# Three of eight pairs of k tiles by seven block products, two of a quad's weight sums made by adding transfers, banks kept open between chunks

## The chip, the cores and the metric

One NeuronCore of a Trainium2 chip runs the whole program. The metric is device time in microseconds (us), the median of several executions. One more execution is taken with the hardware profiler; the rows below are from that one. TensorE multiplies, VectorE (DVE) and ScalarE (ACT) do the elementwise work, GpSimd (POOL) does little, and SyncE (SP) issues most transfers.

## The reference

The reference is an encoder of two layers on 256 tokens of width 2048, in float32. Each layer has three mixers side by side (a chunked mLSTM, a latent attention, a dilated attention), an output projection, and a feed-forward part:

```python
x = x + jnp.einsum('bse,ed->bsd', y, w_out)
h = rms_norm(x, norm_ff)
u = jax.nn.relu(jnp.einsum('bsd,df->bsf', h, w_ff1))
return x + jnp.einsum('bsf,fd->bsd', u * u, w_ff2)
```

`w_ff1` is 2048 x 8192 and `w_ff2` is 8192 x 2048 in each layer. The change lies in the product with `w_ff2`.

## The kernel before

**Products.** Float32 values are split in two parts of a shorter format, hi and lo, and a product of two of them is three matmuls (hi hi, hi lo, lo hi). The main shape is a 128 x 128 stationary tile of activations with 512 columns of weights moving; the result goes to a PSUM bank of 512 columns. All of these go through the helper `mm` (L200).

**Weights.** The class `Weights` streams all weights in one fixed order (`weight_order`). An item is a 128 x 1024 tile: two k tiles of 128 rows by 512 columns. `load` sends it from HBM into one of three `wst` buffers on SP's queue (L239). `split` makes `whi` (an ACT copy) and `wlo` (a DVE subtraction) in one of four pairs of buffers, and `next` hands them to the matmuls in order, with the splits up to two items ahead. A load into a buffer waits on SP until the item that was in it is split.

**The order of the work** is written out by a planner (`Stream`): it keeps a clock that runs with the matmuls, gives every instruction of the side tasks a cost and a due time, and issues a task's next step between two matmuls when it is due (`pump`). It decides the order of instructions in each engine's queue, nothing else; at run time an engine takes its queue in order and waits for what each instruction needs.

**The feed-forward part** runs in four chunks of 2048 inner columns. A chunk has a first half (FF1: 16 tiles of `w_ff1`, two items each, with `ff1_end` for the activation) and a second (FF2: the product with its part of `w_ff2`). The 16 k tiles of FF2 make eight pairs `kp`, the outputs make four groups `g` of 512 columns, and two groups are done together, `left` and `right`, for both token tiles. Fast chunks (three of layer 0, four of layer 1; `fast`) do pairs 2 and 5 (`FAST`) in another way: the 256 x 256 block of activations and the 256 x 1024 block of weights are cut in 2 x 2, and seven products with sums of blocks take the place of eight. I call this a quad. Its activation sums come from `act_sums` in FF1. Its weights are two loaded items, "first" (the pair of the left group) and "second" (that of the right), and two made ones, "sums" and "more sums": four sums of 512 columns, made by four DVE additions (tile `ws`) in `split`. Of the seven products four go to banks of their own (`fast`, L200), the others straight to left and right. `fast_end` adds those four to the x tiles, with eight DVE additions and an ACT copy; then `ff2_end` adds left and right.

The order in a group pair was: left 0, 1, quad 2, left 3, 4, quad 5, left 6, 7, then right 0, 1, 3, 4, 6, 7.

Of the kernel before, what the change touches and what calls it, by code (L numbers as in the profile page):

```python
# [10 lines left out]
F32 = mybir.dt.float32  # L11
F32R = mybir.dt.float32r
AF = mybir.ActivationFunctionType
ALU = mybir.AluOpType
# [53 lines left out]

MLA_AT = ((3, 2), (3, 3), (3, 7), (4, 3), (5, 0), (6, 1))
MARGIN = 0.3  # L70
ML_AT_ONCE = 2
WARM = 14

# [148 lines left out]
class Weights:  # L222
# [2 lines left out]

    def __init__(self, c, items):
        self.c, self.items = c, items
        self.srcs = [(i, src, n) for i, (src, n, kind) in enumerate(items) if src is not None]
        self.st, self.hl = {}, {}
        self.i = self.d = self.k = 0  # L230

    def load(self):
        c = self.c
        if self.d == len(self.srcs):
            return
        i, src, n = self.srcs[self.d]
        self.st[i] = c.wp.tile([P, 1024], F32, tag="wst", name="wst", bufs=c.B_ST)
        for cols in self.pieces(i):
            c.nc.sync.dma_start(self.st[i][:, cols], src[:, cols])  # L239
        self.d += 1  # L240

    def pieces(self, i):

# [3 lines left out]
    def split(self):  # L247

        c, nc, k = self.c, self.c.nc, self.k
        src, n, kind = self.items[k]  # L250
        hi = c.wp.tile([P, 1024], F32R, tag="whi", name="whi", bufs=c.B_HL)
        lo = c.wp.tile([P, 1024], F32R, tag="wlo", name="wlo", bufs=c.B_HL)
        if kind == "sums":
            a, b = self.st.pop(k - 2), self.st.pop(k - 1)

            x, y = (c.big.tile([P, 1040], F32, tag="big", name="ws") for _ in range(2))
            self.st[k + 1] = y
            pieces, st = [slice(0, 512), slice(512, 1024)], x
        else:
            st = self.st[k] if kind else self.st.pop(k)  # L260
            if kind == "second":
                st = st[:, 512:]
                pieces = [slice(0, 512)]
            elif kind == "more sums":
                st = self.st.pop(k)
                pieces = [slice(0, 512), slice(512, 1024)]
            else:
                pieces = self.pieces(k)

        def parts():  # L270
            if kind == "sums":
                t1, t2, t3, t4 = x[:, :512], x[:, 512:1024], y[:, :512], y[:, 512:1024]
                for out, p, q in ((t3, b[:, :512], b[:, 512:]), (t1, a[:, :512], b[:, :512]), (t2, t3, a[:, :512]),
                                  (t4, t2, a[:, 512:])):
                    nc.vector.tensor_tensor(out=out, in0=p, in1=q, op=ALU.add)
                yield
            for cols in pieces:
                nc.scalar.copy(hi[:, cols], st[:, cols])
            yield
            for cols in pieces:  # L280
                nc.vector.tensor_tensor(out=lo[:, cols], in0=st[:, cols], in1=hi[:, cols].bitcast(F32),
                                        op=ALU.subtract)

        t = c.s.spawn(parts())
        if kind != "more sums":
            c.s.step(t)
        else:
            t.due = max(t.due, self.sums.due)
        if kind == "sums":
            self.sums = t  # L290
        self.hl[k] = (hi, lo, t)
        self.k += 1

    def next(self):
        while self.k < min(len(self.items), self.i + self.c.B_HL - 1):
            loads = self.items[self.k][0] is not None
            self.split()
            if loads:
                self.load()
        hi, lo, t = self.hl.pop(self.i)  # L300
        self.c.s.finish(t)
        self.i += 1
        return hi, lo

FAST = (2, 5)


def fast(l, ch, depth):  # L310
    return l == depth - 1 or ch < NCHUNK - 1


def weight_order(c, depth):
    srcs = []
    for l in range(depth):
        for g in range(9):
            for kp in range(KT // 2):
                if g == 1:
                    srcs.append((c.w_in1[l, kp], 2 * G1_W))  # L320
                else:
                    srcs.append((c.w_in[l, g - (g > 1), kp], 1024))
                srcs += [(c.w_mla[l, h], 832) for h, at in enumerate(MLA_AT) if at == (g, kp)]
        srcs += [(c.w_out[l, g, kp], 1024) for g, kps in OUT_ORDER for kp in kps]
        for ch in range(NCHUNK):
            srcs += [(c.w_ff1[l, ch * KT + i, half], 1024) for i in range(KT) for half in range(2)]
            if not fast(l, ch, depth):
                srcs += [(c.w_ff2[l, ch, g, kp], 1024) for g in range(NX) for kp in range(KT // 2)]
                continue
            for g in range(0, NX, 2):  # L330
                for kp in range(KT // 2):
                    if kp in FAST:
                        srcs += [(c.w_ff2[l, ch, g, kp], 1024, "first"), (c.w_ff2[l, ch, g + 1, kp], 1024, "second"),
                                 (None, 1024, "sums"), (None, 1024, "more sums")]
                    else:
                        srcs.append((c.w_ff2[l, ch, g, kp], 1024))
                srcs += [(c.w_ff2[l, ch, g + 1, kp], 1024) for kp in range(KT // 2) if kp not in FAST]
    return [(*a, None)[:3] for a in srcs]


# [232 lines left out]
def layer_tables(c):  # L573

    nc = c.nc
    vec = c.vec
    rope = c.cp.tile([P, 4, NT, MLA_ROPE], F32, tag="rope", name="rope", bufs=1)
    drope = c.cp.tile([P, 2, NT, 4, DIL_ROT], F32, tag="drope", name="drope", bufs=1)
    cs64 = c.const[:, C_C64:C_C64 + 2 * NT * MLA_ROPE].rearrange("p (a t d) -> p a t d", a=2, t=NT)
    cs32 = c.const[:, C_C32:C_C32 + 2 * NT * DIL_ROT].rearrange("p (a t d) -> p a t d", a=2, t=NT)  # L580
    for i in range(4):
# [82 lines left out]
def k_rope(c, z1):  # L664
# [15 lines left out]
    for tt in range(NT):  # L680
        transpose(c, tp[:MLA_ROPE, tt * P:(tt + 1) * P], kr[:, tt])

    kh = c.cp.tile([P, S], F32R, tag="krh", name="krh", bufs=1)
    kl = c.cp.tile([P, S], F32R, tag="krl", name="krl", bufs=1)
    nc.scalar.activation(kl[MLA_ROPE:], c.const[MLA_ROPE:, :S], AF.Copy, scale=0.0)
    yield
    k = tp[:MLA_ROPE, :S]
# [203 lines left out]
def ml_gates(c, z1):  # L891
# [57 lines left out]
                                 op0=ALU.min, op1=ALU.min)  # L949
    yield  # L950

    ahl = c.cp.tile([P, 2, S], F32R, tag="ml_ahl", name="ml_ahl", bufs=1)
    A2 = A.unsqueeze(1).to_broadcast([64, 2, S])
    nc.scalar.copy(ahl[:64], A2)
    nc.vector.tensor_tensor(out=ahl[64:], in0=A2, in1=ahl[:64].bitcast(F32), op=ALU.subtract)
# [167 lines left out]

def mixers(c, prepare, after):
    nc, s = c.nc, c.s
    dv = c.cp.tile([P, 2 * NT * DIL_H * DIL_DH], F32R, tag="dv", name="dv", bufs=1)
    dv = dv.rearrange("p (i t d) -> p i t d", i=2, t=NT)
    c.dv = {(i, tt): dv[:, i, tt] for i in range(2) for tt in range(NT)}
# [95 lines left out]
def ffn(c, l, last_layer, depth):  # L1224

    nc = c.nc
    nxt = [None] * KT
    c.xss = new_ss(c)
    for ch in range(NCHUNK):
        us = [None] * KT  # L1230
        quick = fast(l, ch, depth)
# [4 lines left out]
        for f in range(KT):  # L1236
# [4 lines left out]
            c.s.spawn(ff1_end(c, ps, f, us, uf[kp][:, i * S:(i + 1) * S] if kp in uf else None))  # L1241
            if i and kp in uf:
                c.s.spawn(act_sums(c, us, kp, uf[kp], hls, sums))
        for g in range(0, NX, 2):
            last = last_layer and ch == NCHUNK - 1 and g == NX - 2
            if quick:
                fast_groups(c, us, sums, l, ch, g, last, last_layer, nxt)
                continue
            for gg in (g, g + 1):
                ps = two_banks(c)  # L1250
# [22 lines left out]
    sums[kp] = [(hl[:, i * P:(i + 1) * P], hl[:, 512 + i * P:512 + (i + 1) * P]) for i in range(4)]  # L1273


def fast_groups(c, us, sums, l, ch, g, last, last_layer, nxt):

    def u(kt, tt):
        return us[kt][:, tt * P:(tt + 1) * P], us[kt][:, S + tt * P:S + (tt + 1) * P]
# [6 lines left out]

    one, two = slice(0, 512), slice(512, 1024)
    left, right = two_banks(c), None
    banks = None
    for kp in range(KT // 2):  # L1290
        if kp not in FAST:
            token_group(c, us, left, 512, [kp])
            continue
        first, end = kp == FAST[0], kp == FAST[-1]
        if first:
            right = two_banks(c)
            c.s.until(lambda: c.s.room["m"] >= 4)
            c.s.give(m=-4)
            banks = [new_bank(c, "fast") for _ in range(4)]
        p1, q5, p6, p7 = banks  # L1300
        c.s.until(lambda: kp in sums)
        s1, s2, s3, s4 = sums[kp]
        w = c.w.next()
        product(p1, u(2 * kp, 0), w, one, first, end)
        product(left[0], u(2 * kp + 1, 0), w, two, False, False)
        w = c.w.next()
        product(right[0], s4, w, one, first, False)
        w = c.w.next()
        product(q5, s1, w, one, first, end)
        product(p6, s2, w, two, first, end)  # L1310
        w = c.w.next()
        product(p7, s3, w, one, first, end)
        product(left[1], u(2 * kp + 1, 1), w, two, False, False)
        if end:
            done = c.s.spawn(fast_end(c, banks, g))
    c.s.spawn(ff2_end(c, left, g, l, ch, last_layer, nxt, done))
    kps = [kp for kp in range(KT // 2) if kp not in FAST]
    token_group(c, us, right, 512, kps[:-1] if last else kps, opened=(0,))
    if last:
        last_unit(c, us, right, 512)  # L1320
    c.s.spawn(ff2_end(c, right, g + 1, l, ch, last_layer, nxt, done))


def fast_end(c, banks, g):
# [265 lines left out]
```

## Time and profile before

| | |
|---|---|
| median of 3 runs | 2104.84 us (2104.66 to 2107.78) |
| the profiled execution | 2104.86 us, of which the span from first to last instruction is 2103.1 us |
| busy: PE, DVE, ACT, POOL | 2092.9, 1583.1, 1127.3, 14.0 us |
| moved | 389.91 MB, 185 GB/s on average |

The profile's page gives busy times of the engines, the DMA queues and the chain of waits that ended last. PE is TensorE's matmuls, PEld its weight loads. A stage is read by asking for the busy times of a stretch of the span; a wait is put down to the instruction that came last.

### The profile page before, as it was taken

How to read it: one execution, taken by the hardware profiler on the slowest of the kernel's cores; microseconds unless marked ns; L12 is line 12 of the kernel's file. 1: busy time of each engine (PE TensorE's matmuls, PEld its weight loads, DVE VectorE, ACT ScalarE, POOL GpSimd, SP SyncE). 2: the span in 40 equal slices, each digit the busy share in tenths (PEclk: the TensorE clock that was granted, in tenths of full speed). 3: DMA queues.
4: the chain of work that ended last, by engine and by line, in shares of the span. 5: the costliest groups of instructions: out<-in, count | busy, mean ns of one | idle time of the engine just before them, and what ended most of it. 6: DMA issues, size and time to landing. Idle time of an engine off the chain costs nothing.

```text
span 2103.1 us, 29314 instructions
## 1 busy us (share of the span) xinstructions
PE 2092.9 (100%) x10800; PEld 1790.8 (85%) x10800; DVE 1583.1 (75%) x2624; ACT 1127.3 (54%) x1870; POOL 14.0 (1%) x35
## 2 busy tenths in 40 slices
PE   9999999999999999999999999999999999999999
PEld 8888888888888888888888888888888888888887
DVE  6788865788778778765557888667887787787787
ACT  6777654454455444544456675554544554554453
POOL 1000000000000000001000000000000000000000
PEclk9999999999999999999999999999999999999999
DMA  7554455666656665666555445556666566666665
GB/s 259 167 173 153 150 171 180 194 189 204 191 183 200 200 191 183 210 192 199 179 172 171 139 139 160 175 180 192 192 204 191 179 205 202 186 191 207 187 194 180
DMA packets 109151, 389.91 MB, mean 185 GB/s; under 512 B 12368, under 2 KB 12496, under 8 KB 108752
## 3 DMA queue, kind: packets, MB, share of 16 engines
q1 hardware_dynamic: 107136, 384.71, 58.3%
q10 hardware_dynamic: 1872, 3.33, 0.4%
q8 instruction: 84, 1.38, 0.3%
q14 instruction: 59, 0.48, 0.1%
HBM read 385.90 MB, written 2.10 MB: 184 GB/s over the span
## 4 chain that ended last, share of the span: by engine, by line
PE 96%; DVE 1%; DMA 1%; ACT 1%; issue 0%; ACTq 0%; DVEq 0%
PE g L200 86%; PE fast L200 4%; PE mla_z L200 2%; DMA wst<-w_in 1%; PE oT L200 1%; DVE wlo L104 1%; PE mla_s L200 1%; ACT whi L104 1%; PE ml_h L200 1%; PE pT L206 1%; PE xT L206 0%; PE dil_s L200 0%; PE nkT L206 0%; PE dqkT L206 0%; PE ml_w L200 0%
## 5 line engine op out<-in xcount | busy, mean ns | idle before, releaser
L104 DVE TENSOR_TENSOR wlo<-wst,whi 128x1024 fp32r<-128x1024 f32 (+3 forms) x733 | 864.0, 1189 | 128.1 <-ACT whi L104 126.1
L104 ACT CAST whi<-wst 128x1024 fp32r<-128x1024 f32 (+3 forms) x733 | 748.9, 1024 | 394.0 <-DMA wst<-w_ff 154.1
L200 PE MATMUL g<-whi,u 128*128 128x512 f32 x1712 | 539.1, 389 | 0.0
L200 PE MATMUL g<-xg,whi 128*128 128x512 f32 x2048 | 489.8, 391 | 0.0
L200 PEld LDWEIGHTS g<-xg,whi 128*128 128x128 f32 x2048 | 376.4, 188 | 72.8
L200 PEld LDWEIGHTS g<-whi,u 128*128 128x128 f32 x1712 | 321.4, 188 | 66.7
L200 PE MATMUL g<-whi,xg 128*128 128x512 f32 (+1 forms) x1152 | 370.4, 388 | 0.5 <-ACT whi L104 0.5
L200 PE MATMUL g<-wlo,u 128*128 128x512 f32 x856 | 333.0, 389 | 0.0
L200 PEld LDWEIGHTS g<-xg,wlo 128*128 128x128 f32 x2048 | 262.8, 191 | 11.8 <-ACT xg L104 2.0
L200 PE MATMUL g<-xg,wlo 128*128 128x256 f32 x2048 | 267.3, 283 | 1.1 <-ACT xg L104 1.1
L200 PEld LDWEIGHTS g<-whi,xg 128*128 128x128 f32 x1152 | 214.3, 188 | 37.7 <-ACT whi L104 0.6
L200 PE MATMUL g<-wlo,xg 128*128 128x512 f32 (+1 forms) x576 | 220.8, 383 | 2.5 <-DVE wlo L104 2.5
L104 ACT COPY junk<-g 128x256 f32<-128x256 f32 x128 | 47.8, 374 | 303.5 <-PE g L200 303.5
L200 PEld LDWEIGHTS g<-wlo,u 128*128 128x128 f32 x856 | 160.7, 188 | 33.1
L104 DVE TENSOR_TENSOR junk<-g,junk 128x256 f32<-128x256 f32 x128 | 54.4, 425 | 172.4 <-ACT junk L104 172.4
L200 PE MATMUL g<-whi,y 128*128 128x512 f32 x512 | 164.5, 394 | 0.0
L200 PEld LDWEIGHTS g<-wlo,xg 128*128 128x128 f32 x576 | 108.6, 189 | 21.2 <-DVE wlo L104 4.8
L200 PEld LDWEIGHTS g<-whi,y 128*128 128x128 f32 x512 | 96.2, 188 | 19.5
L200 PE MATMUL g<-wlo,y 128*128 128x512 f32 x256 | 99.8, 390 | 0.0
L104 DVE TENSOR_TENSOR x<-g,x 128x512 f32<-128x512 f32 x80 | 53.4, 688 | 53.7 <-PE g L200 53.7
L104 ACT CAST whi<-ws 128x512 fp32r<-128x512 f32 x112 | 64.0, 619 | 41.1 <-PE g L200 41.1
L104 DVE TENSOR_TENSOR wlo<-ws,whi 128x512 fp32r<-128x512 f32 x112 | 71.6, 688 | 3.3 <-ACT whi L104 1.1
(244 smaller groups left out, 1694.6 us busy)
## 6 DMA issues: line engine op xcount, KB each, us to landing
wst<-w_ff SPq DMA_DIRECT2D x512, 512.0 KB, 4.2
wst<-w_in SPq DMA_DIRECT2D x127, 512.0 KB, 3.7
wst<-w_out SPq DMA_DIRECT2D x64, 512.0 KB, 4.2
wst<-w_in SPq DMA_DIRECT2D x16, 336.0 KB, 3.0
wst<-w_mla SPq DMA_DIRECT2D x12, 416.0 KB, 3.1
x<-x SPq DMA_DIRECT2D x2, 1024.0 KB, 6.5
out<-x ACTq DMA_DIRECT2D x8, 256.0 KB, 2.4
xt<-xT SPq DMA_DIRECT2D x7, 256.0 KB, 6.0
```

The lines of the kernel that those rows point to most:

```text
L104: return fn(*args, **kw)
L200: c.nc.tensor.matmul(out, lhsT, rhs, start=start, stop=stop)
L206: c.nc.tensor.transpose(out, src, c.ident[:n, :n])
```

## The change

- `FAST` becomes (1, 3, 5), three quads in a group pair. The order in the pair is written out (`FAST_ORDER`): left 0, quad 1, left 2, right 0, quad 3, left 4, right 2, quad 5, left 6, 7, right 4, 6, 7.
- A quad's two blocks are loaded in four halves into tiles of the pool `big`, arranged so that w11 and w22 are "first" and w12 and w21 "second". Plain loads keep the three `wst` buffers for themselves. Pairs are loaded up to 12 items (`AHEAD`) ahead of the split, at most two at a time.
- Of the four sums two (t1, t3) are made by transfers: SP loads w22 once more into a half of a `mix` tile, and two transfers issued by POOL add a second block from HBM to what is in the buffer. DVE makes the other two (t2, y) with two additions, due ten us (`LANDING`) after the loads on the planner's clock.
- The sums' tiles take the place of tiles that are free in the feed-forward part: the rope tables, the latent attention's shared keys and one mLSTM tile now lie in the same buffers, `mix0` and `mix1`; y uses the two `mla_zs` buffers.
- The groups' order alternates between chunks (0, 2 and 2, 0). Where a chunk ends with the group pair that the next begins with, the four quad banks stay open (`held`) and `fast_end` runs once for both. This is so at five places (two in layer 0, three in layer 1).
- The left group's output addition waits for `fast_end` only in the last chunk.

```diff
+LANDING = 10.0
+AHEAD = 12
...
+        if kind == "second":
+            self.sum[i] = t = c.s.spawn(self.add(i, self.items[i - 1][0], src))
+            c.s.step(t)
+            t.due = c.s.clk + LANDING
+
+    def loads(self):
+        while self.pairs and self.pairs[0][0] < self.k + AHEAD and self.out["pair"] < 2:
+            self.load(self.pairs)
+            self.load(self.pairs)
+        while self.plain and self.out["plain"] < self.c.B_ST:
+            self.load()
+
+    def add(self, i, first, second):
+        nc = self.c.nc
+        a, b = self.st[i - 1], self.st[i]
+        self.mix = 1 - getattr(self, "mix", 1)
+        x = self.c.cp.tile([P, 1024], F32, tag=f"mix{self.mix}", name="ws", bufs=1)
+        y = self.c.zp.tile([P, 2 * WZ], F32, tag="mla_zs", name="ws")[:, :512]
+        t1, t2, t3 = b[:, :512], x[:, :512], x[:, 512:]
+        nc.sync.dma_start(t3, first[1])
+        nc.gpsimd.dma_start(t1, first[0], accum_op=ALU.add)
+        nc.gpsimd.dma_start(t3, second[0], accum_op=ALU.add)
+        self.st[i + 1], self.st[i + 2] = (t1, t3), (t2, y)
+        yield
+        nc.vector.tensor_tensor(out=t2, in0=t3, in1=a[:, :512], op=ALU.add)
+        nc.vector.tensor_tensor(out=y, in0=t2, in1=b[:, 512:1024], op=ALU.add)
...
-                for out, p, q in ((t3, b[:, :512], b[:, 512:]), (t1, a[:, :512], b[:, :512]), (t2, t3, a[:, :512]),
-                                  (t4, t2, a[:, 512:])):
-                    nc.vector.tensor_tensor(out=out, in0=p, in1=q, op=ALU.add)
...
-FAST = (2, 5)
+FAST = (1, 3, 5)
+FAST_ORDER = ('l0', 'b1', 'l2', 'r0', 'b3', 'l4', 'r2', 'b5', 'l6', 'l7', 'r4', 'r6', 'r7')
...
+def pairs_order(l, ch, depth):
+    return (2, 0) if ch % 2 and fast(l, ch, depth) else (0, 2)
+
+def goes_on(l, ch, g, depth):
+    return (ch + 1 < NCHUNK and fast(l, ch, depth) and fast(l, ch + 1, depth) and pairs_order(l, ch, depth)[1] == g
+            and pairs_order(l, ch + 1, depth)[0] == g)
...
+            first, end = kp == FAST[0], kp == FAST[-1] and not hold
+            if first:
+                right = two_banks(c)
+                if banks is None:
+                    c.s.until(lambda: c.s.room["m"] >= 4)
+                    c.s.give(m=-4)
+                    banks = [new_bank(c, "fast") for _ in range(4)]
+            new = first and held is None
...
+            w = c.w.next()
+            product(p1, u(2 * kp, 0), w, one, new, end)
+            product(right[0], s4, w, two, first, False)
+            w = c.w.next()
+            product(left[0], u(2 * kp + 1, 0), w, one, False, False)
+            w = c.w.next()
+            product(q5, s1, w, one, new, end)
+            product(p7, s3, w, two, new, end)
+            w = c.w.next()
+            product(p6, s2, w, one, new, end)
+            product(left[1], u(2 * kp + 1, 1), w, two, False, False)
```

## Rows read from the trace of the kernel before

**Rows 1.** The page: busy us (share of span) x instructions; granted clock by slice.
```profile
PE 2092.9 (100%) x10800; PEld 1790.8 (85%) x10800; DVE 1583.1 (75%) x2624; ACT 1127.3 (54%) x1870; POOL 14.0 (1%) x35
...
PEclk9999999999999999999999999999999999999999
```

**Rows 2.** The page: shares of the chain that ended last, by engine and by line.
```profile
PE 96%; DVE 1%; DMA 1%; ACT 1%; issue 0%; ACTq 0%; DVEq 0%
PE g L200 86%; PE fast L200 4%; PE mla_z L200 2%; DMA wst<-w_in 1%; PE oT L200 1%; DVE wlo L104 1%; PE mla_s L200 1%; ACT whi L104 1%; PE ml_h L200 1%; PE pT L206 1%; PE xT L206 0%; PE dil_s L200 0%; PE nkT L206 0%; PE dqkT L206 0%; PE ml_w L200 0%
```

**Rows 3.** Waits of TensorE, whole run: for whom, us in total, times, longest us.
```profile
PE g L200 <- DVE wlo L104: 2.5, 4, 0.9
```

**Rows 4.** Busy us by stage: FF1 and FF2 of a chunk, its first group pair.
```profile
core 0: us, PE busy (x) PEld busy (x) DVE busy (x) ACT busy (x) POOL busy (x), PEclk, DMA share, GB/s
357.00:446.60 89.60, 89.04 (x517) 78.63 (x516) 66.78 (x112) 44.99 (x69) 0.00 (x0) 1.00 0.61 187
446.60:531.00 84.40, 84.40 (x374) 69.91 (x373) 70.60 (x90) 42.28 (x52) 0.00 (x0) 1.00 0.65 201
446.60:488.80 42.20, 42.20 (x188) 34.95 (x187) 35.05 (x46) 21.52 (x27) 0.00 (x0) 1.00 0.66 200
```

**Rows 5.** The chain in order of time, 440 to 510 us: start, us, what.
```profile
454.25 2.04 PE fast L200 x9
...
464.45 2.04 PE fast L200 x9
...
496.41 2.04 PE fast L200 x9
```

**Rows 6.** Groups by shape in one group pair's FF2: busy us, mean ns.
```profile
L104 DVE TENSOR_TENSOR wlo<-wst,whi 128x1024 fp32r<-128x1024 f32 x13 | 15.8, 1222 | 3.5 <-ACT whi L104 3.5
L104 ACT CAST whi<-wst 128x1024 fp32r<-128x1024 f32 x14 | 14.7, 1053 | 14.5 <-DMA wst<-w_ff 7.5 <-PE g L200 6.8
...
L104 DVE TENSOR_TENSOR wlo<-ws,whi 128x512 fp32r<-128x512 f32 x8 | 5.1, 689 | 0.1
L104 ACT CAST whi<-ws 128x512 fp32r<-128x512 f32 x8 | 4.6, 619 | 2.8 <-PE g L200 2.8
...
L104 DVE TENSOR_TENSOR ws<-ws,wst 128x512 f32<-128x512 f32 x4 | 2.8, 689 | 0.1
```

**Rows 7.** Tile sf (activation sums): duration ns min/median/max, first and last start.
```profile
L104 DVE TENSOR_TENSOR sf<-uf x28: 283/285/285, 394.3 to 1996.4; 128x128 f32<-128x128 f32 x28
...
L104 DVE TENSOR_TENSOR s_hl<-sf,s_hl x14: 684/685/685, 398.4 to 1999.9; 128x512 fp32r<-128x512 f32 x14
```

**Rows 8.** Timeline, first quad, DVE and then PE: start, us, instruction.
```profile
453.14 2.49 DVE L104 TENSOR_TENSOR wlo<-ws,whi 128x512 fp32r<-128x512 f32 x4
...
454.32 0.39 PE L200 MATMUL fast<-wlo,s_hl 128*128 128x512 f32 x1
...
455.00 0.39 PE L200 MATMUL fast<-wlo,s_hl 128*128 128x512 f32 x1
...
455.68 0.39 PE L200 MATMUL fast<-wlo,s_hl 128*128 128x512 f32 x1
...
456.36 0.39 PE L200 MATMUL g<-wlo,u 128*128 128x512 f32 x1
```

**Rows 9.** DMA of the first 30 us: rate in 40 slices.
```profile
GB/s 0 0 85 229 287 314 336 268 350 374 361 421 396 415 399 396 377 374 358 350 382 358 337 342 341 405 418 407 432 392 388 365 130 120 269 161 0 0 54 151
```

**Rows 10.** Waits of SP's queue in one chunk's FF2.
```profile
SPq L239 <- DVE wlo L104: 46.7, 24, 3.3
```

**Rows 11.** The DMA issues: count, KB each, median us to landing.
```profile
wst<-w_ff SPq DMA_DIRECT2D x512, 512.0 KB, 4.2
...
out<-x ACTq DMA_DIRECT2D x8, 256.0 KB, 2.4
xt<-xT SPq DMA_DIRECT2D x7, 256.0 KB, 6.0
...
wst<-w_in SPq DMA_DIRECT2D x2, 256.0 KB, 3.7
```

**Rows 12.** The chain in order of time at the end of the run.
```profile
2099.24 0.69 DVE x L104
```

**Rows 13.** Timeline of POOL: rope tables of the two layers.
```profile
24.89 1.73 POOL L104 TENSOR_TENSOR rope<-const,vec 128x128 f32<-128x128 f32 x4
...
991.36 2.90 POOL L104 TENSOR_TENSOR rope<-const,vec 128x128 f32<-128x128 f32 x4 [959.84 <-DMA vec<-vecs]
```

More of the change, by code (lines that the diff above doesn't have):

```diff
@@ L227, in __init__ @@
         self.c, self.items = c, items
[L228 to L232, printed above, removed]
-        c = self.c
[L234 to L240, printed above, removed]
+        srcs = [(i, *item) for i, item in enumerate(items) if item[0] is not None]
@@ new lines, in __init__, with load @@
+        self.plain, self.pairs = ([a for a in srcs if bool(a[3]) == k] for k in (False, True))
+        self.st, self.hl, self.sum = {}, {}, {}
+        self.out = dict(plain=0, pair=0)
+        self.i = self.k = 0
+    def load(self, srcs=None):
+        c = self.c
+        i, src, n, kind = (srcs or self.plain).pop(0)
+        if kind:
+            self.st[i] = c.big.tile([P, 1040], F32, tag="big", name="wab")
+        else:
+            self.st[i] = c.wp.tile([P, 1024], F32, tag="wst", name="wst", bufs=c.B_ST)
+        self.out["plain"] += not kind
+        self.out["pair"] += kind == "first"
+        if kind:
+            for j, half in enumerate(src):
+                c.nc.sync.dma_start(self.st[i][:, j * 512:j * 512 + 512], half)
+        else:
+            for cols in self.pieces(i):
+                c.nc.sync.dma_start(self.st[i][:, cols], src[:, cols])
+        if kind == "second":
+            self.sum[i] = t = c.s.spawn(self.add(i, self.items[i - 1][0], src))
+            c.s.step(t)
+            t.due = c.s.clk + LANDING
@@ L252, in split @@
         lo = c.wp.tile([P, 1024], F32R, tag="wlo", name="wlo", bufs=c.B_HL)
[L253 to L258, printed above, removed]
-        else:
[L260 to L268, printed above, removed]
@@ L270, in parts @@
-        def parts():
-            if kind == "sums":
-                t1, t2, t3, t4 = x[:, :512], x[:, 512:1024], y[:, :512], y[:, 512:1024]
-                for out, p, q in ((t3, b[:, :512], b[:, 512:]), (t1, a[:, :512], b[:, :512]), (t2, t3, a[:, :512]),
-                                  (t4, t2, a[:, 512:])):
-                    nc.vector.tensor_tensor(out=out, in0=p, in1=q, op=ALU.add)
-                yield
-            for cols in pieces:
-                nc.scalar.copy(hi[:, cols], st[:, cols])
+        if kind and "sums" in kind:
+            c.s.finish(self.sum[k - 1 - (kind != "sums")])
@@ L279, in parts @@
+        st = self.st.pop(k)
+        if kind and "sums" in kind:
+            n = 1024 // len(st)
+            pieces = [(slice(i * n, i * n + n), p) for i, p in enumerate(st)]
+        elif kind == "second":
+            pieces = [(slice(0, 512), st[:, 512:1024])]
+        else:
+            pieces = [(cols, st[:, cols]) for cols in self.pieces(k)]
+        def parts():
+            for cols, p in pieces:
+                nc.scalar.copy(hi[:, cols], p)
             yield
-            for cols in pieces:
-                nc.vector.tensor_tensor(out=lo[:, cols], in0=st[:, cols], in1=hi[:, cols].bitcast(F32),
-                                        op=ALU.subtract)
+            for cols, p in pieces:
+                nc.vector.tensor_tensor(out=lo[:, cols], in0=p, in1=hi[:, cols].bitcast(F32), op=ALU.subtract)
@@ L284, in split @@
         t = c.s.spawn(parts())
-        if kind != "more sums":
+        if kind and "sums" in kind:
+            t.due = max(t.due, max(self.sum[k - 1 - (kind != "sums")].last.values()))
+        else:
             c.s.step(t)
[L287 to L290, printed above, removed]
+        self.out["plain"] -= not kind
+        self.out["pair"] -= kind == "more sums"
         self.hl[k] = (hi, lo, t)
@@ L295, in next @@
         while self.k < min(len(self.items), self.i + self.c.B_HL - 1):
-            loads = self.items[self.k][0] is not None
             self.split()
-            if loads:
-                self.load()
+            self.loads()
         hi, lo, t = self.hl.pop(self.i)
@@ L329, in weight_order @@
                 continue
[L330 to L333, printed above, removed]
+            for g in pairs_order(l, ch, depth):
+                for at in FAST_ORDER:
+                    kp = int(at[1])
+                    if at[0] == "b":
+                        (w11, w21), (w12, w22) = ([c.w_ff2[l, ch, g + j, kp][:, h:h + 512] for h in (0, 512)]
+                                                  for j in range(2))
+                        srcs += [((w11, w22), 1024, "first"), ((w12, w21), 1024, "second"),
                                  (None, 1024, "sums"), (None, 1024, "more sums")]
                     else:
-                        srcs.append((c.w_ff2[l, ch, g, kp], 1024))
-                srcs += [(c.w_ff2[l, ch, g + 1, kp], 1024) for kp in range(KT // 2) if kp not in FAST]
+                        srcs.append((c.w_ff2[l, ch, g + (at[0] == "r"), kp], 1024))
     return [(*a, None)[:3] for a in srcs]
@@ L576, in layer_tables @@
     vec = c.vec
-    rope = c.cp.tile([P, 4, NT, MLA_ROPE], F32, tag="rope", name="rope", bufs=1)
-    drope = c.cp.tile([P, 2, NT, 4, DIL_ROT], F32, tag="drope", name="drope", bufs=1)
+    tab = c.cp.tile([P, 1024], F32, tag="mix0", name="rope", bufs=1)
+    rope = tab[:, :512].rearrange("p (a t d) -> p a t d", a=4, t=NT)
+    drope = tab[:, 512:].rearrange("p (a t h d) -> p a t h d", a=2, t=NT, h=4)
     cs64 = c.const[:, C_C64:C_C64 + 2 * NT * MLA_ROPE].rearrange("p (a t d) -> p a t d", a=2, t=NT)
@@ L681, in k_rope @@
         transpose(c, tp[:MLA_ROPE, tt * P:(tt + 1) * P], kr[:, tt])
-    kh = c.cp.tile([P, S], F32R, tag="krh", name="krh", bufs=1)
-    kl = c.cp.tile([P, S], F32R, tag="krl", name="krl", bufs=1)
+    kh, kl = c.mix[:, :S], c.mix[:, S:2 * S]
     nc.scalar.activation(kl[MLA_ROPE:], c.const[MLA_ROPE:, :S], AF.Copy, scale=0.0)
@@ L950, in ml_gates @@
     yield
-    ahl = c.cp.tile([P, 2, S], F32R, tag="ml_ahl", name="ml_ahl", bufs=1)
+    ahl = c.mix[:, 2 * S:].rearrange("p (i s) -> p i s", i=2)
     A2 = A.unsqueeze(1).to_broadcast([64, 2, S])
@@ L1125, in mixers @@
     nc, s = c.nc, c.s
+    c.mix = c.cp.tile([P, 1024], F32R, tag="mix1", name="mix", bufs=1)
     dv = c.cp.tile([P, 2 * NT * DIL_H * DIL_DH], F32R, tag="dv", name="dv", bufs=1)
@@ L1228, in ffn @@
     c.xss = new_ss(c)
+    held = None
     for ch in range(NCHUNK):
@@ L1243, in ffn @@
                 c.s.spawn(act_sums(c, us, kp, uf[kp], hls, sums))
-        for g in range(0, NX, 2):
-            last = last_layer and ch == NCHUNK - 1 and g == NX - 2
+        for n, g in enumerate(pairs_order(l, ch, depth)):
+            last = last_layer and ch == NCHUNK - 1 and n == 1
             if quick:
-                fast_groups(c, us, sums, l, ch, g, last, last_layer, nxt)
+                held = fast_groups(c, us, sums, l, ch, g, last, last_layer, nxt, held, goes_on(l, ch, g, depth))
                 continue
@@ L1273, in act_sums, with fast_groups @@
     sums[kp] = [(hl[:, i * P:(i + 1) * P], hl[:, 512 + i * P:512 + (i + 1) * P]) for i in range(4)]
-def fast_groups(c, us, sums, l, ch, g, last, last_layer, nxt):
+def fast_groups(c, us, sums, l, ch, g, last, last_layer, nxt, banks, hold):
     def u(kt, tt):
@@ L1288, in fast_groups @@
     left, right = two_banks(c), None
-    banks = None
-    for kp in range(KT // 2):
-        if kp not in FAST:
-            token_group(c, us, left, 512, [kp])
[L1293 to L1320, printed above, removed]
+    done, held = None, banks
+    for n, at in enumerate(FAST_ORDER):
+        kp = int(at[1])
+        more = [b[0] for b in FAST_ORDER[n + 1:]]
+        if at[0] == "b":
+            first, end = kp == FAST[0], kp == FAST[-1] and not hold
[6 more added lines that the diff above has]
+            new = first and held is None
+            p1, q5, p6, p7 = banks
+            c.s.until(lambda: kp in sums)
+            s1, s2, s3, s4 = sums[kp]
+            w = c.w.next()
[9 more added lines that the diff above has]
+            product(left[1], u(2 * kp + 1, 1), w, two, False, False)
+            if end:
+                done = c.s.spawn(fast_end(c, banks, g))
+        elif at[0] == "l":
+            token_group(c, us, left, 512, [kp])
+            if "l" not in more:
+                c.s.spawn(ff2_end(c, left, g, l, ch, last_layer, nxt, done if ch == NCHUNK - 1 else None))
+        elif last and not more:
+            last_unit(c, us, right, 512)
+        else:
+            token_group(c, us, right, 512, [kp], opened=(0,))
@@ L1321, in fast_groups @@
     c.s.spawn(ff2_end(c, right, g + 1, l, ch, last_layer, nxt, done))
+    return banks if hold else None
 def fast_end(c, banks, g):
```

## The prediction

> **What bounds the kernel now.** I read the busy shares first: TensorE is busy for 2092.9 of the 2103.1 us span, at the full granted clock (1.00 of 2.4 GHz) in every slice [rows 1]. A busy TensorE need not be at its peak, so the chain of waits comes next: 96% of it is TensorE, and the helper of the block products alone (L200, tiles g and fast) makes 89% [rows 2]. The list of what TensorE waited for shows that these matmuls are not late: the longest entry is 2.5 us in 4 waits in the whole run [rows 3]. The table by stage shows the second feed-forward half (FF2) of one chunk without a gap, 84.40 us busy of 84.40 [rows 4]. There only the number of matmuls times their pitch sets the time. The pitch comes from the chain in order of time: nine fast matmuls take 2.04 us, so 0.2267 us each, and the same quad of the next group of outputs starts 42.16 us later, which is exactly 186 of them [rows 5]. What the reader is to see: a removed matmul is worth 0.2267 us, as long as no operand of the rest comes late.
>
> **Matmuls removed.** Seven chunks are fast (three of layer 0, four of layer 1), with two groups of 1024 outputs each: 14 groups. Before, two of eight pairs of k tiles take seven block products instead of eight; after, three. Each more quad saves one product of three 512-column matmuls: 14 x 3 = 42 matmuls, 10800 to 10758, and 42 x 0.2267 = 9.52 us. A group goes from 186 to 183 matmuls, 41.48 us. All of it lies on the path. No edit adds a matmul; that the change doesn't do this is no rival, as the count can be read off the order of blocks.
>
> **DVE and ACT.** From the FF2 window by shape [rows 6]: one more quad per group adds splits of one 1024 tile (1.22), one 512 (0.69) and four 512 (2.76) and drops two plain 1024 tiles: +2.2 us on DVE, and by the same count 1.05 + 4 x 0.62 + 0.62 - 2.11 = +2.0 on ACT. The adds go from eight to six 512-column additions, -1.4. DVE's 35.0 us of a 42.2 us group [rows 4] become some 36 of 41.5. Held banks drop fast_end (eight DVE additions, 5.5 us) in five groups of 14. The third set of activation sums costs 4 x 0.285 + 0.69 = 1.8 us of DVE and 0.62 of ACT in each FF1 [rows 7], where DVE works 66.8 of 89.6 us [rows 4]. I cost all this at nothing: TensorE's matmuls hide it. Without that cover the price is what a late remainder costs in a quad, and the cover is thin there: in the first quad the four remainders of the sums were computed from 453.14 to 455.63 and read by matmuls at 454.32, 455.00, 455.68 and 456.36 [rows 8], 0.5 to 0.7 us ahead. The bank change only takes waits away; the right group's banks now go in use one block earlier, but the output addition that frees them (two of 0.69 us) starts with the last matmul of the group and has some 3.4 us.
>
> **Transfers added.** Each of the 42 quads issues, beside its two blocks (now four transfers of 256 KB), one more 256 KB load on SP and two adding transfers on POOL's queue. A group's payload goes from 8.4 MB to 10 x 0.52 + 3 x (1.05 + 0.79) = 10.8 MB in 41.5 us, 259 GB/s against 200 [rows 4]. The first 30 us of the run show slices at 350 to 432 GB/s [rows 9], so the rate alone costs nothing, even with the 1.6 MB of destinations read again (some 300 GB/s).
>
> **The wait added.** DVE's two additions of a quad wait for the adding transfers, and everything behind them in DVE's queue waits along: remainders that TensorE needs. This is the one step that can cost more than the change gives. Take zero at the start of the group's first quad. The third quad's pair is loaded when the first quad's last sums are split, 1.36 on the planner's clock; its additions are due ten us later, 11.36, and are so queued ahead of the second quad's remainders (that quad starts at 4.76 + 5.44 = 10.20). TensorE reads those 2.27 us after 10.20, and before them DVE has 1.38 us of additions and 0.69 of the first remainder to do: the additions must start by 10.4. The transfers: the 256 KB load overwrites the mix tile, so SP holds it until the first quad's t2 is split (ACT 2 x 0.62, DVE 0.69 [rows 6], from a weight buffer that comes free at 0): 2.0. Behind it in SP's queue stand two plain loads that are read some 10 us later; SP spends long stretches on such waits today (46.7 us in a chunk's FF2 [rows 10]) with no gap in TensorE. Then this load and one adding transfer on top of it, in series. No row shows an adding transfer; the nearest are the plain ones of 256 KB: 2.4 us (a store, nothing beside it), 3.7 (half a weight tile), 6.0 (in the crowded start) [rows 11]. I take 3.7 for both, the load of the same kind of rows from the same memory: 2.0 + 7.4 = 9.4, 1.0 us in time. With 2.4 it is 3.6 us in time; with 6.0 3.6 us late. By the same count the next group's first quad lands at 13.6 + 7.4 = 21.0 and is due at 21.96 inside the third quad: 1.0 us in time again. These are 14 + 7 = 21 exposed additions; the other 21 fall among plain tiles or in FF1, where a split tile waits for its matmuls far longer. At 3.7 the term is zero; its ends are 0 and 21 x 3.6 = +76 us.
>
> A rule of the Trainium skill puts it shorter (DMA: Bandwidth & Descriptors, "Anatomy of one DMA"): some 2.0 us fixed and the bytes at 436 GB/s for a transfer from GpSimd, 2.6 us for 256 KB by that page as an estimate; no row here shows it, and the sum would be the same.
>
> **The sum.** Against the profiled execution: 2104.86 us, of which the span is 2103.1; 2104.86 - 9.52 = 2095.34. The median of the runs is 2104.84, so the same number holds for it: **2095.3 us**, 0.45% faster. A measurement of this kernel can tell 0.2%, 4.2 us, from no change. The other ends: start and tail are the same instructions (after the last matmul one output addition of 0.69 us and the store [rows 12]), and since TensorE has no gap in FF2 there is next to nothing else to win; 1.5 us of stalls elsewhere that could shift give the lower bound 2093.5.
>
> **Rivals.** *Adding transfers late; slower.* If load and addition take 4.85 us each (between 3.7 and 6.0), they land at 11.7, 1.3 us late, TensorE stands 1.3 us in 21 quads, 28 us: **2123 us**. It decides from 21 x late = 9.52, that is 0.45 us late or 4.4 us for each transfer. For it: an adding transfer reads its destination too, the two of a quad stand one behind the other on POOL, and loads of 512 KB take 4.2 us in this stage already [rows 11]. Against it: half the bytes, and SP's order lets the pair's own loads go out earlier than I counted. 0.14.
>
> *POOL held up by DVE.* POOL's four rope products took 1.73 us in one place and 2.90 in another [rows 13], so something beside it slows it. If the issue of an adding transfer waits out one DVE instruction in progress, 1.22 us [rows 6], the landing is at 10.6, 0.25 late: 21 x 0.25 = 5.2 us given back, **2100.5**. The Trainium skill (SBUF — State Buffer, "Who interferes with whom") has a rule for this: a DVE instruction with two inputs in SBUF holds up a GpSimd instruction that reads SBUF until it ends, and DVE's FF2 work is nearly all such additions; the page only infers that writing descriptors is free of it. The slower rope rows fit that rule, but no run so far has a transfer issued by POOL. 0.14.
>
> *DVE backlog.* In the seven groups that follow a fast_end in the same chunk, 5.5 us of fast_end and 2.8 of output additions stand ahead of a quad that now comes after one plain tile, not two. If remainders there slip by the 0.9 us of the longest such wait [rows 3], 7 x 0.9 = 6.3 us come back: **2101.6**, no change to speak of. Against it: two additions of each quad are gone from this spot. 0.10.
>
> **How the numbers follow.** Forecast 0.62, late transfers 0.14, POOL held up 0.14, backlog 0.10. Faster by over 0.2% (under 2100.6): the forecast, two thirds of POOL held up, and a little of the backlog: 0.73. Within 0.2% (to 2109.0): the rest of both and transfers that are just late, 0.14. Slower: 0.13. The range goes from 2093.5 through the two small rivals and late transfers up to 0.6 us (21 x 0.6 = 12.6): to 2108.
>
> **What would show it.** Right: 10758 matmuls, the same quad of the next group 41.48 us later, TensorE busy for all of an FF2 stage. Additions of the sums on DVE that wait under a microsecond on a transfer; loads plus adding transfer under 8.4 us together. Wrong: an entry of TensorE waiting for DVE's remainders in the quads, some 21 or 42 times, with DVE waiting for transfers ahead of it; TensorE's stage table under its full length; plain loads far above 4.2 us.

## The result, and the profile after

The changed kernel takes **2225.98 us** (median of 4 runs, 2213.58 to 2226.43) against 2105.32 us for the kernel before on the same occasions: ratio 1.0556, interval 1.0531 to 1.0582. I forecast 2095.3, faster. The rival of late adding transfers (2123 us, chance 0.14) had the mechanism and the sign, but not the size.

The page of the changed kernel (busy us, granted clock, the new DMA queue, and the DMA issues with KB and median us to landing) answers to [rows 1, 11]:

```profile
PE 2129.1 (96%) x10758; PEld 1803.9 (81%) x10758; DVE 1571.8 (71%) x2647; ACT 1152.9 (52%) x1928; POOL 86.6 (4%) x119
...
PEclk9999999999999999999999999999999999999999
...
q0 software_dynamic: 12096, 22.03, 5.7%
...
wst<-w_ff SPq DMA_DIRECT2D x428, 512.0 KB, 4.4
...
ws<-w_ff SPq DMA_DIRECT2D x42, 256.0 KB, 3.5
wab<-w_ff POOLq DMA_DIRECT2D x42, 256.0 KB, 6.2
ws<-w_ff POOLq DMA_DIRECT2D x42, 256.0 KB, 7.1
```

The 42 matmuls are gone (10758), and plain loads are hardly slower (4.4 us, 4.2 before). But the adding transfers land in 6.2 and 7.1 us, where the prediction took 3.7 and had 6.0 as its worst. The list of waits (who waited for whom: us, times, longest) shows what that does; before, TensorE's longest entry was 2.5 us [rows 3]:

```profile
DVE ws L108 <- DMA ws<-w_ff: 152.4, 33, 6.8
...
PE fast L204 <- DVE wlo L108: 59.3, 21, 3.8
...
PE g L204 <- DVE wlo L108: 25.7, 17, 3.8
```

DVE waits 152 us for the buffers that the transfers add into, TensorE 85 us for DVE's remainders. Of these 85 us, 20.0 lie in FF1, as the pages show for its matmuls with the remainders (the changed kernel, then the one before; idle time and what ended it stand last):

```profile
L204 PE MATMUL g<-xg,wlo 128*128 128x256 f32 x2048 | 272.8, 286 | 21.1 <-DVE wlo L108 20.0
```

```profile
L200 PE MATMUL g<-xg,wlo 128*128 128x256 f32 x2048 | 267.3, 283 | 1.1 <-ACT xg L104 1.1
```

Most of the rest of the loss is clock. TensorE is busy for 45.7 us more than 2092.9 - 9.5 = 2083.4, and 85.0 + 45.7 = 130.7 us is the distance from the forecast to the result. The mean granted clock over the span of 2224.4 us is 0.983 (1.000 before), which I estimate at 38 of the 45.7 us (0.017 x 2224.4); the other 8 us are not accounted for. The table by stage (us, PE busy, granted clock, DMA share, GB/s) of stretches of 4 us in the first FF2 shows where the clock falls:

```profile
472.00:476.00 4.00, 4.00 (x18) 1.00 0.77 235
...
480.00:484.00 4.00, 2.88 (x13) 1.00 1.04 311
484.00:488.00 4.00, 2.42 (x7) 0.79 0.36 71
488.00:492.00 4.00, 4.00 (x15) 0.78 1.07 331
492.00:496.00 4.00, 4.00 (x20) 1.00 0.75 210
```

A gap of 2.70 us in TensorE's work ends at 485.58. The mean of the stretch in which it ends is 0.79 of 2.4 GHz and that of the next 0.78, so a part of each runs at 1.2, and it is back to 1.00 in the last. The 40 slices of the page, in tenths, hide this.

One quad in order of time. The first fast quad starts at 456.0. This is the chain of the changed kernel (start, us, what):

```profile
457.65 3.02 DMA ws<-w_ff
460.67 0.03 issue
460.69 0.04 POOLq L277
460.73 0.48 issue
461.23 7.46 DMA ws<-w_ff
468.69 0.02 issue
468.71 0.70 DVE ws L108
```

and, in the timelines, DVE's queue and TensorE's over the same time:

```profile
460.99 1.82 DVE L108 TENSOR_TENSOR wlo<-wab,whi 128x1024 fp32r<-128x1024 f32 x2
468.71 1.42 DVE L108 TENSOR_TENSOR ws<-ws,wab 128x512 f32<-128x512 f32 x2 [5.90 <-DMA ws<-w_ff]
470.05 0.68 DVE L108 TENSOR_TENSOR wlo<-wab,whi 128x512 fp32r<-128x512 f32 x1
470.65 1.89 DVE L108 TENSOR_TENSOR wlo<-ws,whi 128x512 fp32r<-128x512 f32 x3
...
468.26 0.39 PE L204 MATMUL fast<-whi,s_hl 128*128 128x512 f32 x1
470.78 0.50 PE L204 MATMUL fast<-wlo,s_hl 128*128 128x512 f32 x1 [2.13 <-DVE wlo L108]
...
485.58 0.50 PE L204 MATMUL fast<-wlo,s_hl 128*128 128x512 f32 x1 [2.70 <-DVE wlo L108]
```

The third load goes out 1.6 us after the quad's start (I counted 2.0) and lands in 3.0 (3.7); POOL issues the second adding transfer 0.6 us after that (not in the sum), and it takes 7.5 (3.7). It lands 12.7 us after the quad's start, where I had 9.4. DVE stands idle 5.9 us for it with the second quad's remainders behind, and TensorE stops in the middle of that quad. The additions for which DVE waits belong to a third quad, some 10 us later: nothing needs them yet.

### The profile page after: what moved, and what is told of

Read it like the earlier page. It is cut to its first block, busy times and chain, and to the rows that moved or that the text cites. A ratio compares the mean times of both kernels' runs of the same rounds, so it can differ in the third digit from the quotient of the medians.

```text
span 2224.4 us, 29741 instructions
## 1 busy us (share of the span) xinstructions
PE 2129.1 (96%) x10758; PEld 1803.9 (81%) x10758; DVE 1571.8 (71%) x2647; ACT 1152.9 (52%) x1928; POOL 86.6 (4%) x119
## 4 chain that ended last, share of the span: by engine, by line
PE 65%; DMA 18%; DVE 11%; issue 3%; ACT 2%; POOL 0%; SPq 0%; DVEq 0%; POOLq 0%; ACTq 0%
PE g L204 57%; DMA ws<-w_ff 13%; DVE wlo L108 7%; DMA wst<-w_ff 3%; PE fast L204 2%; DMA wst<-w_in 2%; PE mla_z L204 2%; DVE ws L108 1%; ACT whi L108 1%; DVE junk L108 1%; DMA wab<-w_ff 1%; PE oT L204 1%; DVE x L108 1%; PE mla_s L204 1%; PE ml_h L204 0%
## 5 line engine op out<-in xcount | busy, mean ns | idle before, releaser
L108 DVE TENSOR_TENSOR wlo<-wst,whi 128x1024 fp32r<-128x1024 f32 (+2 forms) x649 | 774.0, 1207 | 157.1 <-ACT whi L108 151.7
L108 ACT CAST whi<-wst 128x1024 fp32r<-128x1024 f32 (+2 forms) x649 | 668.0, 1039 | 333.4 <-DMA wst<-w_ff 181.8
L204 PE MATMUL g<-whi,u 128*128 128x512 f32 x1544 | 503.4, 397 | 1.7 <-DVE x L108 1.7
L204 PEld LDWEIGHTS g<-whi,u 128*128 128x128 f32 x1544 | 297.5, 193 | 65.2 <-issue 2.1
L204 PE MATMUL g<-wlo,u 128*128 128x512 f32 x772 | 308.7, 400 | 2.4 <-DVE wlo L108 2.3
L204 PEld LDWEIGHTS g<-wlo,u 128*128 128x128 f32 x772 | 148.4, 192 | 41.1 <-DVE wlo L108 10.1
L108 ACT CAST whi<-wab 128x512 fp32r<-128x512 f32 (+1 forms) x126 | 96.2, 764 | 157.1 <-PE g L204 73.5
L108 DVE TENSOR_TENSOR ws<-ws,wab 128x512 f32<-128x512 f32 x84 | 58.1, 691 | 158.2 <-DMA ws<-w_ff 152.4
L108 DVE TENSOR_TENSOR wlo<-wab,whi 128x512 fp32r<-128x512 f32 (+1 forms) x126 | 106.2, 863 | 24.0 <-ACT whi L108 24.0
L204 PE MATMUL fast<-wlo,s_hl 128*128 128x512 f32 x126 | 56.4, 448 | 59.3 <-DVE wlo L108 59.3
```

The source lines that it names most:

```text
L108: return fn(*args, **kw)
L204: c.nc.tensor.matmul(out, lhsT, rhs, start=start, stop=stop)
```

## The experiments

**Is it DVE's queue?** Theory A: the order in DVE's queue, additions ahead of remainders, is the loss. Theory B: quads too dense, or transfers that crowd the engines. The first run moves only the due time.

```diff
-LANDING = 10.0
+LANDING = 16.0
```

> Theory A (DVE takes a quad's two additions into its queue before the adding transfers have landed, and the remainders behind them come late): with the additions due 16 us after the loads instead of 10, they stand behind the second quad's remainders, after the landing that the changed kernel's trace shows some 12.7 us after the quad before starts. TensorE's waits for DVE (85 us in the changed kernel) go to under 5, the granted clock returns to 1.00, and the time is 2095 to 2098 us. Theory B (the three quads stand too close for DVE and ACT, or the transfers crowd out the plain loads): the waits stay, over 2150 us.

Measured: 2101.99 us, ratio 0.9980 (0.9971 to 0.9989). The DMA issues and the waits of TensorE:

```profile
wab<-w_ff POOLq DMA_DIRECT2D x42, 256.0 KB, 6.5
ws<-w_ff POOLq DMA_DIRECT2D x42, 256.0 KB, 7.3
```

```profile
PE g L204 <- DVE wlo L108: 3.4, 4, 1.8
PE g L204 <- DVE x L108: 2.6, 3, 1.4
PE g L204 <- ACT xg L108: 1.1, 2, 0.6
```

The transfers are as slow as in the changed kernel, and 124 us are gone, with the granted clock at 0.999. DVE's wait for them is no longer among the sixty longest entries of the list. The time is 4 us above A's window; what is left is the subject of the later runs.

```diff
-LANDING = 10.0
+LANDING = 13.0
```

> Theory A: 13 us lies just behind the landing of 12.7 us as seen from the quad's start (the loads are issued 1.4 us later than that, so the additions are due at 14.4): most waits go, 2095 to 2115 us. If the additions fall back inside a quad here and there, the upper part of that. Theory B: over 2150 us.

2108.83 us, 1.0016 (1.0007 to 1.0025), inside A's window. DVE waits 19.7 us in 19 places here, so 13 is the edge, as the landing at 12.7 us said.

The third run takes the wait away and leaves the order and the 10 us; two of a quad's sums then lack a block:

```diff
-        nc.vector.tensor_tensor(out=t2, in0=t3, in1=a[:, :512], op=ALU.add)
+        nc.vector.tensor_tensor(out=t2, in0=a[:, 512:1024], in1=a[:, :512], op=ALU.add)
```

> The changed kernel with its 10 us; DVE's first addition of a quad reads the two halves of the plainly loaded block instead of the buffer that the transfers add into (t2 and y then lack w12). Transfers, order and work are the same, only DVE's wait for them is gone; ACT still waits for them when it splits t1 and t3. Theory A (it is DVE's queue that stands behind the transfers): the 152 us of DVE's waits and nearly all of TensorE's go, 2098 to 2106 us. Theory B (the sums themselves come late for their matmuls, or the engines are too busy with transfers): over 2180 us.

2101.11 us, 0.9978 (0.9969 to 0.9987), with the transfers at 6.9 and 7.3 us. That settles it: with all transfers in place, all instructions in the same order, and only this operand changed, 125 us go. ACT's own wait for t1 and t3 costs nothing that shows.

**Why are the transfers slow?** Here they write instead of adding, so two of a quad's sums lack a block.

```diff
-        nc.gpsimd.dma_start(t1, first[0], accum_op=ALU.add)
-        nc.gpsimd.dma_start(t3, second[0], accum_op=ALU.add)
+        nc.gpsimd.dma_start(t1, first[0])
+        nc.gpsimd.dma_start(t3, second[0])
```

> The two transfers on POOL's queue write instead of adding (two of the four sums of every quad then lack one block). It tells apart why they are slow. If the adding is (the destination read first): they land in 3 to 4 us instead of 6.2 and 7.1, and with 3 us less the time falls to 2095 to 2110 us. If the path through POOL's queue is: 6 to 7 us stays and the time stays within 1% of 2226 us.

One run of 2146.78 us, between the two theories. Its DMA issues:

```profile
wab<-w_ff SPq DMA_DIRECT2D x168, 256.0 KB, 5.1
ws<-w_ff SPq DMA_DIRECT2D x42, 256.0 KB, 3.5
wab<-w_ff POOLq DMA_DIRECT2D x42, 256.0 KB, 4.8
ws<-w_ff POOLq DMA_DIRECT2D x42, 256.0 KB, 5.6
```

The adding has a part: 6.2 and 7.1 us become 4.8 and 5.6, so 1.4 to 1.5 us are its price. Whether POOL's queue has one is not shown. On SP's queue the same 256 KB take 3.5 us as the third load of a quad and 5.1 as one of the four loads of its blocks, so POOL's plain loads lie within what SP's take in other company. Without the adding DVE still waits 98 us, and TensorE 32 us for remainders, where it waited 85.

**Do the transfers pay at all?** Here DVE makes all four sums, with the quads, order, banks and 10 us of the change:

```diff
-        nc.sync.dma_start(t3, first[1])
-        nc.gpsimd.dma_start(t1, first[0], accum_op=ALU.add)
-        nc.gpsimd.dma_start(t3, second[0], accum_op=ALU.add)
...
+        nc.vector.tensor_tensor(out=t3, in0=a[:, 512:1024], in1=t1, op=ALU.add)
+        nc.vector.tensor_tensor(out=t1, in0=t1, in1=a[:, :512], op=ALU.add)
```

> All four sums by DVE as before, no third load and no adding transfer; quads, order, banks and the 10 us kept. Theory A: the pair's own loads land within 10 us, so nothing waits on a transfer: 2095 to 2100 us, where DVE's 84 more additions (58 us) stay hidden. Theory B: over 2150 us, and DVE's larger share of each group makes it worse than the changed kernel rather than better.

2114.19 us, 1.0043 (1.0030 to 1.0055): A's direction, but 14 us above its window, a miss. The 84 additions do not hide: the run without the wait, with the same 10 us, took 2101.11. TensorE's waits name the place:

```profile
PE g L204 <- DVE x L108: 11.9, 7, 4.2
PE g L204 <- DVE wlo L108: 5.5, 8, 1.9
```

It waits for output additions (x), seven times, as there are seven groups that follow another in the same chunk. These waits are 11.9 of the 21.8 us by which the profiled execution (2117.07 us) lies above 2095.3. So the transfers, with a due time that fits them, are the better way here (2102 against 2114 us); sums by DVE with a later due time were not run.

**What is left above 2095?** The chain of the run with 16 us (its profiled execution, 2105.65 us, is the slowest of eleven) shows nine matmuls of the first quad of a group, and then of the next group's, in the first and in the third chunk, and two plain loads:

```profile
451.14 2.04 PE fast L204 x9
...
473.28 5.98 DMA wst<-w_ff
...
494.16 2.08 PE fast L204 x9
...
649.27 8.90 DMA wst<-w_ff
...
797.68 2.04 PE fast L204 x9
...
839.16 2.04 PE fast L204 x9
```

The first pair is 43.02 us apart instead of 41.48, 1.5 us too much; the last is 41.48, as forecast. So the loss is not the same at each of the seven places. fast_end and the output additions stand there on DVE, and the plain loads took 6.0 and 8.9 us. The next runs each change one thing about it. All but the one with sums by DVE have the additions due at 16 us. The first changes the order of the quads:

```diff
-FAST_ORDER = ('l0', 'b1', 'l2', 'r0', 'b3', 'l4', 'r2', 'b5', 'l6', 'l7', 'r4', 'r6', 'r7')
+FAST_ORDER = ('l0', 'l2', 'b1', 'l4', 'r0', 'b3', 'l6', 'r2', 'b5', 'l7', 'r4', 'r6', 'r7')
```

> Additions due at 16 us, and the order in a group begins with two plain tiles: left 0, 2, quad 1, left 4, right 0, quad 3, left 6, right 2, quad 5, left 7, right 4, 6, 7. Theory A (what is left above 2095 in the run with 16 us, some 7 us, is lost where the next group's first quad follows fast_end and the output additions in the same chunk: about 1.5 us at each of seven places): with a plain tile more ahead of that quad DVE catches up, 2095 to 2099 us. Theory B (the plain loads are late because the adding transfers share the engines with them, wherever the quads stand): 2100 to 2104, as with 16 us alone.

2105.84 us, 1.0004 (0.9995 to 1.0013), with runs from 2100.9 to 2110.2: no better, above both windows, a miss. The next leaves fast_end out:

```diff
 def fast_end(c, banks, g):
...
     yield
-    a, b = junk5(c), junk5(c)
-    nc.scalar.copy(a, p6)
-    yield
-    tt(a, p1, a)
-    tt(x[0][0], p1, x[0][0])
+    yield
     c.s.give(m=2)
```

(and the other six additions left out in the same way, so that four products never reach x)

> Additions due at 16 us; fast_end does nothing, so the four products in banks of their own never reach x. Nine times eight DVE additions and a copy are left out. Theory A (DVE's backlog after a quad): 2094 to 2097 us. Theory B (late plain loads): 2099 to 2103.

2097.45 us, 0.9958 (0.9944 to 0.9972), just above A's window: 4.5 of the 6.7 us come with fast_end. Its DVE additions, its ACT copy and its hold on the four banks went together, so that it is DVE's work is likely, not shown. The order of the quads does not cure it, leaving the work out does. The next closes the banks at the end of each group:

```diff
 def goes_on(l, ch, g, depth):
-    return (ch + 1 < NCHUNK and fast(l, ch, depth) and fast(l, ch + 1, depth) and pairs_order(l, ch, depth)[1] == g
-            and pairs_order(l, ch + 1, depth)[0] == g)
+    return False
```

> Additions due at 16 us; banks closed at the end of each group, fast_end runs 14 times instead of nine. The five more fall where FF1 follows, with DVE at some 75%: theory A (backlog counts only ahead of a quad) within 2 us of the run with 16 us; if keeping banks open matters by itself, 5 x 1.5 = 7 us more, 2107 to 2112.

2102.10 us, 0.9983 (0.9974 to 0.9992): the same as with banks held. The bank part of the change is worth nothing that can be measured, which fits that the fast_ends it drops lie under FF1.

The order of spread16 with DVE sums:

> All four sums by DVE, the 10 us, and the order of the quads with two plain tiles first. The same kernel with the order of the change took 2114 us and waited 12 us for output additions. Theory A (DVE's backlog at the start of a group): 2097 to 2104 us. If DVE is simply too full in these groups (some 39 of 41.5 us), it stays at 2110 to 2116, and moving two sums to transfers is worth its price.

2114.35 us, 1.0040 (1.0026 to 1.0055): as before that move, and TensorE still waits 11.9 us in seven places for output additions. That DVE is too full with six more additions of 0.69 us in each group fits this. The next gives three of fast_end's additions to POOL:

```diff
+    def tp(out, a):
+        nc.gpsimd.tensor_tensor(out=out, in0=out, in1=a, op=ALU.add)
...
-    tt(x[0][1], x[0][1], b)
+    tp(x[0][1], b)
```

(and two more in the same way)

> Additions due at 16 us, and the three additions of fast_end that read and write only SBUF go to POOL (27 of 72). If DVE's backlog of fast_end is what is left (leaving all of fast_end out gave 2097.5 against 2102.0), a part of the 4.5 us comes back: 2098 to 2101. If POOL and DVE hold each other up at their common port, it is no faster, 2102 to 2108.

2107.05 us, 1.0006 (0.9997 to 1.0014): no gain. One such addition takes POOL 1.30 us, DVE 0.68. Whether the two hold each other up or the later x is what costs was not told apart. The last goes back to two quads in a group:

```diff
-FAST = (1, 3, 5)
-FAST_ORDER = ('l0', 'b1', 'l2', 'r0', 'b3', 'l4', 'r2', 'b5', 'l6', 'l7', 'r4', 'r6', 'r7')
+FAST = (1, 5)
+FAST_ORDER = ('l0', 'b1', 'l2', 'r0', 'l3', 'l4', 'r2', 'b5', 'l6', 'l7', 'r3', 'r4', 'r6', 'r7')
```

> Additions due at 16 us, with two quads per group (pairs 1 and 5) instead of three; the matmuls are 10800 again. If the third quad is worth its 9.5 us, less what fast_end takes back, this takes 2105 to 2108 us, as the kernel before. If three quads cost DVE as much as they save, it takes 2100 to 2103.

2118.66 us, 1.0061 (1.0046 to 1.0077), outside both windows. The waits of DVE show that the 16 us suit this order less:

```profile
DVE ws L108 <- DMA ws<-w_ff: 17.9, 8, 3.7
```

TensorE waits 5.4 us in five places for a quad's remainders behind them; the rest of the 13 us above the kernel before is not accounted for. So the run does not price the third quad; it suggests that a due time fits one order only.

## Why the prediction was wrong

**The matmuls removed** held: 10758, and 41.48 us from a quad to that of the next group where nothing is late. With the wait out of the way the gain is 0.2%, not 0.45%.

**The wait added** is the step that failed, and in it one term. "With 2.4 it is 3.6 us in time; with 6.0 3.6 us late" had the right chain and the right victim: load, adding transfer, DVE's additions, the second quad's remainders. The start (1.6 us for 2.0) and the load (3.0 to 3.5 for 3.7) were a little better than taken; the adding transfer was 6.2 to 7.5 us and not 3.7. I took it from a plain load on another queue, "the load of the same kind of rows from the same memory". The run without adding puts 1.4 to 1.5 us on the adding; the 1.1 to 1.9 us that its plain loads take above 3.7 stay open between POOL's queue and the loads beside them. The upper end of 6.0 was a plain load in a crowded stretch and so no bound for a slower kind. The estimate of 2.6 us from the Trainium skill (DMA: Bandwidth & Descriptors, "Anatomy of one DMA") is not borne out here: 4.8 us is the shortest median of POOL's transfers, plain and beside other loads.

**The price of being late** was too low also. The decision point stood in the text, 0.45 us late in 21 places; the quad shown was 2.3 us late, which by that count gives 48 us. The count of places was right: TensorE waits 21 times inside a quad, 59.3 us. The length was not, since lateness is handed on. The second quad's third load goes out 5.7 us after that quad's start (466.22) and not 1.6, as it stands behind the four loads of the pair, and for their buffers SP waits on DVE's late remainders; in the run with 16 us it goes out after 1.4 us (459.30 and 460.71). SP's queue in the changed kernel:

```profile
457.65 0.33 SPq L275 DMA_DIRECT2D ws<-w_ff  x1
...
462.24 9.32 SPq L249 DMA_DIRECT2D wab<-w_ff  x4
471.96 0.33 SPq L275 DMA_DIRECT2D ws<-w_ff  x1
```

The other 21 additions were put at nothing, as they "fall among plain tiles or in FF1". In FF1 they cost 20.0 us, nearly all of it in one wait of 2.0 to 3.8 us near the end of each of the seven that a fast FF2 follows. The chain of the first, ahead of the quads above:

```profile
439.23 7.03 DMA ws<-w_ff
446.25 0.02 issue
446.27 0.70 DVE ws L108
...
447.61 1.23 DVE wlo L108
448.84 0.04 issue
448.88 7.32 PE g L204 x28
```

The clock, which the prediction left out, took some 38 us more; before there was no gap in FF2 from which to read it.

**Of the other rivals**, DVE's backlog has support: 4.5 us by leaving out fast_end, where I had 6.3. That the issue on POOL waits out a DVE instruction of 1.22 us is not seen. With plain loads the 42 issues of the second transfer take 536 to 544 ns each, in the run without adding (shortest, median, longest):

```profile
L277 POOL DMA_DIRECT2D ws<-w_ff x42: 536/536/544, 416.2 to 2107.0; - x42
```

What holds the transfer between issue and landing no run tells.

**Costed at nothing:** no run shows a price for act_sums or ACT's splits; fast_end had one. The rate of the transfers is not cleared, as the chain of the run with 16 us goes through two slow plain loads.

## What to carry to other kernels

An instruction that waits on a transfer costs what stands behind it in its queue, not what needs its result: place it by the measured landing, with a margin, and where nothing urgent follows. Here the number 10 in place of 16 turned a gain of 0.2% into a loss of 5.6%. When a kind of transfer has never run in the kernel, its price has no upper end from other kinds; a plan that breaks at 4.4 us when the nearest rows lie at 2.4 to 6.0 is a toss, not a forecast.

## What was not expected of the hardware

A 256 KB transfer that adds into SBUF takes 6.2 to 7.1 us from POOL's queue beside other loads, about twice the 3.5 us of a quad's plain third load on SP. A gap of 2.13 us of TensorE left the granted clock at 1.00; after one of 2.70 us, 15 us later, it was 0.79 and 0.78 in two stretches of 4 us. Over the run the 85 us of waits cost some 38 us more in this way.
